# Two column blocks of the shared values by seven half-size products instead of eight

## The chip, the cores and the metric

The kernel runs on one core of a Trainium2 chip. The metric is the time of one launch in microseconds, as the median of several runs. The engines are named as in the profile: PE multiplies matrices into PSUM, DVE (VectorE) and ACT (ScalarE) work on tiles, POOL does next to nothing here, and SP issues most of the DMAs (ACT issues a few).

## The reference

A trunk of two layers over 512 tokens (T) of width 2048 (D), all in float32. Layer 0 is differential attention. After it the stream `x` is projected once to shared keys, values and forget-gate logits, and layer 1 (forgetting attention) reads these.

```python
def shared_kv(x, c_act, w_mod_kv, b_mod_kv, w_kv, b_f):
    mod = c_act @ w_mod_kv + b_mod_kv
    shift, scale = jnp.split(mod, 2, axis=-1)
    hk = x * (1.0 + scale[:, None]) + shift[:, None]
    kvf = hk @ w_kv
    k, v, zf = jnp.split(kvf, [B_WIDTH, 2 * B_WIDTH], axis=-1)
    ...
```

Each layer also has `mod = c_act @ w_mod[l] + b_mod[l]`, which gives a shift, a scale and a gate of the stream, and ends in `x <- LN(alpha * x + gate * mixer(x * (1 + scale) + shift))`.

## The kernel before

**A product.** Every projection is done as three matmuls (`products`): each operand is split into a rounded upper part (fp32r) and the rest, and upper x upper, upper x lower and lower x upper are summed in PSUM. The operand of the shared projection, `hk`, lies turned (features on the 128 partitions, P) in 16 pairs of tiles `Hh[kt]`, `Hl[kt]` of 128 x 512 tokens. `n` is the layer-normed stream of layer 0, four blocks of 128 tokens (TB).

**The weights** come through `WeightStream`. A step is two rows of 128 weights, up to 512 columns wide (512 KB). SP loads it into one of four `wst` buffers; ACT casts it to `whi` (L113) and DVE subtracts to get `wlo` (L114), three buffers of each. `get(job, s, ahead=2)` prepares the steps two ahead of the one that PE uses.

**A group** (`group`) multiplies one block of up to 512 columns: eight weight steps, in each of which PE goes over the four token blocks ("banks"), a burst of 6 matmuls for each. A whole step is 24 matmuls. With `natural` the tokens are PE's stationary side, which gives values; without it the weights are, which gives turned keys.

**The values**, `vj[0]` to `vj[4]`, are columns 0, 512 and 1024 (512 wide), 1536 and 1800 (264 wide; the last 16 are the gate logits). `vj[0]` is computed while its operands are being built: a build of half the tokens is transposes on PE, four activations on ACT (L1347, L1348) and DVE's subtractions (L1349), or, where the tokens were turned by way of a DRAM tile (`turned`), ACT's L1332 and DVE's L1331 and L1333. The turned tokens are kept in the place where `n` lay, for the later operands of layer 1 (`build_h`, L1384, in kj[3]). `vj[1]` to `vj[4]` follow as plain groups, then the keys `kj[0]` to `kj[3]`, then layer 1's own projections, `bj`.

**Background work.** `mod_stream` sums the modulation rows on DVE, a 128x512 block of weights at a time (L433, `macc<-ms`). `bg` says after which bursts one such product is done: after every second in the values, after three of four in the keys, after two of three in part of layer 0's output projection. Its blocks come through three `ms` buffers, loaded two ahead; those whose number lies in `deep` go to free tiles of the key pool (`msk`) and are loaded up to seven ahead.

**Order.** A scheduler puts each engine's instructions in order from the written program; each engine, and each issuing queue, then goes through its list and waits in place for what an instruction needs.

## Time and profile before

| | |
|---|---|
| median of 3 runs | 1925.03 us (1924.69 to 1926.31) |
| span of the profiled execution | 1923.5 us |
| PE busy / DVE / ACT | 99% / 71% / 38% of the span |
| matmuls on PE | 8921 |
| granted TensorE clock | full throughout |
| DMA traffic | 382.22 MB, 199 GB/s on average, 385 GB/s in the fullest of 40 slices |
| vj[0] with the build / vj[1] / vj[2] | 965 to 1022 / 1022 to 1064 / 1064 to 1107 us |
| vj[3] / vj[4] / kj[0] to kj[3] | 1107 to 1131 / 1131 to 1154 / 1154 to 1329 us |

Busy shares are over the whole span. PE's matmuls overlap, so their listed durations (0.39 us) are longer than the distance of their starts, and a busy PE isn't a proof that it waits for nothing; its gaps are seen in the windows. A row of the groups ends with the idle time of the engine just ahead of the group's instructions and with what ended it.

### The profile page before, as it was taken

The page shows a single profiled execution, that of the slowest core. Times are in us where ns is not written, and L with a number is a line of the kernel's source. Part 1 is how long each engine was busy: PE and PEld are TensorE (multiplying, and loading weights), DVE is VectorE, ACT ScalarE, POOL GpSimd, SP SyncE. Part 2 cuts the span into 40 slices and gives each one's busy share as a digit, 9 for nine tenths or more (in the row PEclk, how much of TensorE's full clock was granted, in tenths as well). Part 3 has the DMA queues.
Part 4 walks back from the last instruction along what each step waited for, and adds up shares of the span by engine and source line. Part 5 has one row for each costly group of instructions (what it writes and reads, how often), then busy time and mean ns, then how long its engine had stood idle before and what let it go on. Part 6 is the DMA issues. An engine that isn't in the chain of part 4 may idle for free.

```text
span 1923.5 us, 25879 instructions
## 1 busy us (share of the span) xinstructions
PE 1910.4 (99%) x8921; PEld 1593.5 (83%) x8921; DVE 1370.3 (71%) x2617; ACT 732.9 (38%) x1266; POOL 2.3 (0%) x11
## 2 busy tenths in 40 slices
PE   8999999999999999999999999999999999999998
PEld 7888888888888888888888898888888888888887
DVE  8993578777676868667675477777566666686768
ACT  3656344333232344521272232224344444453122
POOL 0000000000000000000000000000000000000000
PEclk9999999999999999999999999999999999999999
DMA  9993566676767675476557586775355555555622
GB/s 346 385 333 95 160 186 196 213 234 196 228 203 224 207 223 180 122 241 222 179 165 256 181 294 211 258 258 160 114 149 156 161 149 160 154 154 170 224 93 110
DMA packets 352275, 382.22 MB, mean 199 GB/s; under 512 B 77912, under 2 KB 256244, under 8 KB 351376
## 3 DMA queue, kind: packets, MB, share of 16 engines
q1 hardware_dynamic: 349040, 376.23, 62.2%
q10 hardware_dynamic: 3104, 4.35, 0.6%
q8 instruction: 70, 1.15, 0.3%
q14 instruction: 61, 0.50, 0.1%
HBM read 348.68 MB, written 31.80 MB: 198 GB/s over the span
## 4 chain that ended last, share of the span: by engine, by line
PE 97%; DVE 1%; SPq 1%; DMA 0%; issue 0%; ACT 0%; ACTq 0%
PE acc L208 27%; PE acc L210 27%; PE acc L209 27%; PE acc L720 4%; PE sc L720 2%; PE sc L210 1%; PE sc L209 1%; PE sc L208 1%; PE o L208 1%; PE o L210 1%; PE o L209 1%; PE o L720 1%; SPq L568 0%; PE tr L686 0%; PE tr L660 0%; DMA sms<-in_w_mod_dram 0%
## 5 line engine op out<-in xcount | busy, mean ns | idle before, releaser
L113 ACT CAST whi<-wst 128x1024 fp32r<-128x1024 f32 (+2 forms) x298 | 303.4, 1018 | 617.6 <-PE acc L210 310.1
L114 DVE TENSOR_TENSOR wlo<-wst,whi 128x1024 fp32r<-128x1024 f32 (+2 forms) x298 | 351.4, 1180 | 248.8 <-ACT whi L113 228.9
L208 PE MATMUL acc<-hh,whi 128*128 128x512 f32 x1184 | 462.9, 391 | 0.0
L209 PE MATMUL acc<-hl,whi 128*128 128x512 f32 x1184 | 461.6, 390 | 0.0
L210 PE MATMUL acc<-hh,wlo 128*128 128x512 f32 x1184 | 460.0, 390 | 0.0
L208 PE MATMUL acc<-whi,hh 128*128 128x512 f32 (+1 forms) x1104 | 418.5, 379 | 0.0
L209 PE MATMUL acc<-wlo,hh 128*128 128x512 f32 (+1 forms) x1104 | 416.7, 377 | 0.0
L210 PE MATMUL acc<-whi,hl 128*128 128x512 f32 (+1 forms) x1104 | 416.2, 377 | 0.0
L433 DVE SCALAR_TENSOR_TENSOR macc<-ms,cact,macc 128x512 f32<-128x512 f32 x307 | 229.0, 746 | 63.0 <-DMA ms<-in_w_mod_dram 44.5
L210 PEld LDWEIGHTS acc<-hh,wlo 128*128 128x128 f32 x1184 | 222.3, 188 | 47.4
L208 PEld LDWEIGHTS acc<-hh,whi 128*128 128x128 f32 x1184 | 222.3, 188 | 44.0 <-DVE sgb L1509 0.8
L209 PEld LDWEIGHTS acc<-hl,whi 128*128 128x128 f32 x1184 | 222.5, 188 | 42.3
L210 PEld LDWEIGHTS acc<-whi,hl 128*128 128x128 f32 x1104 | 207.3, 188 | 38.9
L208 PEld LDWEIGHTS acc<-whi,hh 128*128 128x128 f32 x1104 | 207.3, 188 | 37.2 <-DVE ztmp L1241 0.6
L209 PEld LDWEIGHTS acc<-wlo,hh 128*128 128x128 f32 x1104 | 207.4, 188 | 36.0
L618 DVE SCALAR_TENSOR_TENSOR sacc<-sms,cact,sacc 128x512 f32<-128x512 f32 (+1 forms) x128 | 89.9, 703 | 4.6 <-DMA sms<-in_w_mod_dram 0.7
L904 ACT ACTIVATE e<-e,mn 128x128 f32<-128x128 f32 (+3 forms) x64 | 36.0, 563 | 109.5 <-DVE mn L900 102.9
L1559 ACT ACTIVATE eb<-eb,mnb 128x128 f32<-128x128 f32 (+1 forms) x64 | 35.9, 561 | 72.7 <-DVE mnb L1556 72.4
L720 PE MATMUL acc<-wlo,hh 128*128 128x512 f32 x128 | 49.8, 398 | 0.0
L720 PE MATMUL acc<-whi,hl 128*128 128x512 f32 x128 | 49.3, 393 | 0.0
L720 PE MATMUL acc<-whi,hh 128*128 128x512 f32 x128 | 49.2, 393 | 0.0
L132 DVE TENSOR_TENSOR wlo<-wst,whi 128x768 fp32r<-128x768 f32 (+1 forms) x32 | 34.8, 1088 | 17.8 <-ACT whi L125 16.5
(336 smaller groups left out, 2096.6 us busy)
## 6 DMA issues: line engine op xcount, KB each, us to landing
wst<-in_a_w_in_dram SPq DMA_DIRECT2D x240, 256.0 KB
ms<-in_w_mod_dram SPq DMA_DIRECT2D x136, 256.0 KB
ms<-in_kv_w_mod_dram SPq DMA_DIRECT2D x64, 512.0 KB
wst<-in_b_w_in_dram SPq DMA_DIRECT2D x128, 256.0 KB
sms<-in_w_mod_dram SPq DMA_DIRECT2D x56, 512.0 KB
wst<-in_kv_w_dram SPq DMA_DIRECT2D x56, 512.0 KB
ms<-in_w_mod_dram SPq DMA_DIRECT2D x32, 512.0 KB
wst<-in_a_w_out_dram SPq DMA_DIRECT2D x32, 512.0 KB
```

What stands on the lines that cost most here:

```text
L113: self.nc.scalar.copy(hi[:, :, :w], st[:, :, :w])
L114: self.nc.vector.tensor_tensor(lo[:, :, :w], st[:, :, :w], hi[:, :, :w].bitcast(F32), op=ALU.subtract)
L132: self.nc.vector.tensor_tensor(lo[:, :, :w], st[:, :, :w], hi[:, :, :w].bitcast(F32), op=ALU.subtract)
L208: PE.matmul(dst, lhs[0], rhs[0], start=start, stop=False, skip_group_check=True)
L209: PE.matmul(dst, lhs[0], rhs[1], start=False, stop=False, skip_group_check=True)
L210: PE.matmul(dst, lhs[1], rhs[0], start=False, stop=stop, skip_group_check=True)
L433: ins = V.scalar_tensor_tensor(acc, w, cact[:, kt : kt + 1], acc, op0=ALU.mult, op1=ALU.add)
L618: V.scalar_tensor_tensor(acc, w, sc, acc, op0=ALU.mult, op1=ALU.add)
L720: PE.matmul(bank[n, bk], l, r, start=start, stop=stop, skip_group_check=True)
L904: S.activation(e[:, :w], e[:, :w], AF.Exp, bias=mn, scale=-1.0, accum_out=rs)
L1559: S.activation(e[:, :w], e[:, :w], AF.Exp, bias=mn, scale=-1.0, accum_out=rs)
```

## The change

`vj[1]` and `vj[2]` (value columns 512 to 1535) together are a product of 512 tokens x 2048 features by 2048 x 1024. Cut in halves along each side it is eight products of half-size blocks. The change computes it by seven products of sums of blocks (the scheme with fifteen additions known as Strassen-Winograd): the tokens halve into the first and last 256, the features into even and odd tiles `kt`, the columns into the two blocks of 512.

- `combine(s)` makes, for the two feature tiles of weight step s, the four sums of token halves, in DVE (four 128x256 operations) from freshly activated tiles (ACT, L1491; L1488 in halves for s = 6 and 7). For each pair of s, ACT casts the upper parts into `su` (two of L1507), and DVE subtracts the lower parts `sl` (four of L1511). `su` takes the places of `n`, which is split in four tiles by columns: each is stored to `s_dram` (1 MB) ahead and loaded back by `back_n` after the products. `sl` takes the sixteen tiles of the key pool.
- The order is now `vj[0]`, `vj[3]` (with combine(0) to (5)), `vj[4]`, then `seven_products` (with combine(6) and (7)), then the keys.
- `seven_products` goes over the weights twice, in 12 and in 16 steps of 512 KB with 12 matmuls each. In `PairFirst` the last eight steps need one sum of weights (L87, in place, ahead of the cast), in `PairSecond` every two steps need three (L108 to L110).
- Results are combined on ACT and DVE from PSUM at the ends of the passes (L1549 to L1586).
- Background products: none in `seven_products`, after every fourth burst in `vj[3]` and `vj[4]`, after every burst in the keys, after five of six in part of layer 0's output projection; `deep` holds numbers 82 to 137 rather than 50 to 105.
- `n` goes to `n_dram` in sixteen pieces of 256 KB rather than four of 1 MB.

The diff, cut to its core (lines that only pass on the splitting of `n` are left out):

```diff
+class PairFirst:
+
+    width = 512
+    gate = None
+
+    def __init__(self, src, c0, c1):
+        self.src, self.c0, self.c1 = src, c0, c1
+
+    def load(self, nc, dst, kt):
+        n = kt // 2
+        if n < 4:
+            rows = self.src[4 * n * P : (4 * n + 4) * P, self.c0 : self.c0 + 512]
+            nc.sync.dma_start(dst, rows.rearrange("(k u p) n -> p k u n", p=P, u=2)[:, :, 0, :])
+        else:
+            rows = self.src[2 * (n - 4) * P : (2 * (n - 4) + 2) * P, self.c1 : self.c1 + 512]
+            nc.sync.dma_start(dst, rows.rearrange("(k p) n -> p k n", p=P))
+
+    def sums(self, nc, n, st, after):
+        if n >= 4:
+            nc.vector.tensor_tensor(st[:, 0, :], st[:, 1, :], st[:, 0, :], op=ALU.subtract)
+
+class PairSecond:
+
+    width = 512
+    gate = None
+
+    def __init__(self, src, c0, c1):
+        self.src, self.cols = src, (c0, c1)
+
+    def load(self, nc, dst, kt):
+        n = kt // 2
+        c0 = self.cols[n % 2]
+        rows = self.src[2 * (n // 2) * P : (2 * (n // 2) + 2) * P, c0 : c0 + 512]
+        nc.sync.dma_start(dst, rows.rearrange("(k p) n -> p k n", p=P))
+
+    def sums(self, nc, n, st, after):
+        if n % 2 == 0:
+            other, minus = after(), partial(nc.vector.tensor_tensor, op=ALU.subtract)
+            minus(other[:, 0, :], other[:, 0, :], st[:, 0, :])
+            minus(other[:, 1, :], other[:, 1, :], other[:, 0, :])
+            minus(st[:, 0, :], st[:, 1, :], other[:, 1, :])
...
+        if isinstance(job, (PairFirst, PairSecond)):
+            self.load(self.done + 2)
+            job.sums(self.nc, s, st, lambda: self.stage[self.done + 1])
...
+    s_dram = dram.tile([4, P, TB, 512], F32, name="s_dram")
...
+    pair = PairFirst(kv_w, 2048 + 512, 2048 + 1024), PairSecond(kv_w, 2048 + 512, 2048 + 1024)
-    for j in [o[1] for o in oA] + vj + kj + bj + [o[1] for o in oB]:
+    for j in [o[1] for o in oA] + [vj[0], vj[3], vj[4]]:
+        ws.add_job(j)
+    for j, steps in zip(pair, (12, 16)):
+        ws.add_job(j, steps)
+    for j in kj + bj + [o[1] for o in oB]:
...
+    def new_n():
+        nt[:] = [zp[0].tile([P, TB, 512], F32, name="n", tag="n", bufs=4) for _ in range(4)]
...
-            bg = (lambda n: 1 if n % 3 else 0) if layer == 0 and k in (1, 2) else 0
+            bg = (lambda n: 1 if n % 6 else 0) if layer == 0 and k in (1, 2) else 0
...
-            deep=range(50, 106),
+            deep=range(82, 138),
...
-        for c0, c1 in ((0, 256), (256, 1024)) if b == 3 else ((0, 1024),):
-            S.activation(n[:, b, c0:c1], n[:, b, c0:c1], AF.Identity, scale=rstd, bias=mr)
-        V.tensor_scalar(n[:, b, 1024:], n[:, b, 1024:], mv[:, 0:1], rstd, op0=ALU.subtract, op1=ALU.mult)
-        nc.sync.dma_start(n_dram[b * P : (b + 1) * P, :], n[:, b, :])
+        for c0, c1 in ((0, 256), (256, 512), (512, 1024)) if b == 3 else ((0, 512), (512, 1024)):
+            S.activation(ncols(b, c0, c1), ncols(b, c0, c1), AF.Identity, scale=rstd, bias=mr)
+        for c0 in (1024, 1536):
+            row = ncols(b, c0, c0 + 512)
+            V.tensor_scalar(row, row, mv[:, 0:1], rstd, op0=ALU.subtract, op1=ALU.mult)
+        for c0 in range(0, D, 512):
+            nc.sync.dma_start(n_dram[b * P : (b + 1) * P, c0 : c0 + 512], ncols(b, c0, c0 + 512))
...
+    def combine(s):
+
+        cs = 256 * s, 256 * s + 256
+        whole = []
+        for q in range(2):
+            kt = 2 * s + q
+            f = npool.tile([P, T], F32, name="htmp", tag="htmp", bufs=2)
+            sc, sh = ab["kv"][0][:, kt : kt + 1], ab["kv"][1][:, kt : kt + 1]
+            if turned(s, 0):
+                for half in range(2):
+                    to = f[:, 256 * half : 256 * half + 256].rearrange("p (b a c) -> p b a c", b=2, c=32)
+                    S.activation(to, place_n(s, half, q), AF.Identity, scale=sc, bias=sh)
+            else:
+                src = ncols(slice(0, TB), kt * P, (kt + 1) * P)
+                S.activation(f.rearrange("p (b t) -> p b t", t=P), src, AF.Identity, scale=sc, bias=sh)
+            whole.append((f[:, 0:256], f[:, 256:512]))
+        if s % 2:
+            nc.sync.dma_start(s_dram[s // 2], nt[s // 2])
+        sums = npool.tile([P, 4, 256], F32, name="sums", tag="tn", bufs=2)
+        (a11, a21), (a12, a22) = whole
+        s3, s4, s1, s2 = (sums[:, k, :] for k in range(4))
+        V.tensor_tensor(s1, a21, a22, op=ALU.add)
+        V.tensor_tensor(s2, s1, a11, op=ALU.subtract)
+        V.tensor_tensor(s3, a11, a21, op=ALU.subtract)
+        V.tensor_tensor(s4, a12, s2, op=ALU.subtract)
+        waiting.append((s, sums))
+        if s % 2:
+            t = npool.tile([P, 2, 4, 256], F32R, name="su", tag="n", bufs=4)
+            for k, (w, sums) in enumerate(waiting):
+                upper[w] = t[:, k]
+                S.copy(upper[w], sums)
+                lower[w] = [kpool.tile([P, 2, 256], F32R, name="sl", tag="K") for _ in range(2)]
+                for m, lo in enumerate(lower[w]):
+                    two = slice(2 * m, 2 * m + 2)
+                    V.tensor_tensor(lo, sums[:, two], upper[w][:, two].bitcast(F32), op=ALU.subtract)
+            waiting.clear()
...
+    def combined(s, k, b):
+
+        bs = slice(b * P, (b + 1) * P)
+        return upper[s][:, k, bs], lower[s][k // 2][:, k % 2, bs]
...
+    def seven_products():
+
+        one, two = pair
+        c0, c1 = (c - 2048 for c in (one.c0, one.c1))
+        both = range(2)
+
+        def add(dst, lhs, tiles, k, start=False, stop=False):
+            for b in both:
+                products(dst[b], lhs(b), (tiles[0][k], tiles[1][k]), start, stop)
+
+        def store(t, b, col):
+            nc.scalar.dma_start(v_dram[b * P : (b + 1) * P, col : col + 512], t)
+
+        p1 = [acc_bank() for _ in both]
+        for a in range(4):
+            tiles = ws.get(one, a)
+            if a < 2:
+                combine(6 + a)
+            for k in range(2):
+                s = 2 * a + k
+                add(p1, lambda b: plain(2 * s, b), tiles, k, s == 0, s == 7)
+        p2 = [tr_bank("p2"), o_bank("p2")]
+        first = [npool.tile([P, T], F32, name="vfirst", tag="vfirst", bufs=2) for _ in both]
+        for b in both:
+            S.copy(first[b], p1[b])
+        p7 = [acc_bank() for _ in both]
+        p3 = [sc_bank() for _ in both]
+        for s in range(8):
+            tiles = ws.get(one, 4 + s)
+            add(p7, lambda b: combined(s, 0, b), tiles, 0, s == 0, s == 7)
+            add(p3, lambda b: combined(s, 1, b), tiles, 1, s == 0, s == 7)
+        diff = [npool.tile([P, T], F32, name="htmp", tag="htmp", bufs=2) for _ in both]
+        for b in both:
+            S.copy(diff[b], p3[b])
+            V.tensor_tensor(diff[b], p7[b], diff[b], op=ALU.subtract)
+        for s in range(8):
+            last = s == 7
+            ta = ws.get(two, 2 * s, 1)
+            add(p2, lambda b: plain(2 * s + 1, b), ta, 1, s == 0, last)
+            if s not in (0, 7):
+                add(p7, lambda b: plain(2 * s + 1, 2 + b), ta, 0)
+            tb = ws.get(two, 2 * s + 1, 1 if s in (0, 7) else 2)
+            add(p1, lambda b: combined(s, 3, b), tb, 1, stop=last)
+            if s in (0, 7):
+                add(p7, lambda b: plain(2 * s + 1, 2 + b), ta, 0, stop=last)
+            add(p3, lambda b: combined(s, 2, b), tb, 0, stop=last)
+            if last:
+                for b in both:
+                    V.tensor_tensor(first[b], p2[b], first[b], op=ALU.add)
+                    store(first[b], b, c0)
+                us = [ktile("us") for _ in both]
+                for b in both:
+                    S.copy(us[b], p1[b])
+                for b in both:
+                    t = ktile("vt")
+                    V.tensor_tensor(t, p7[b], us[b], op=ALU.add)
+                    store(t, 2 + b, c0)
+                for b in both:
+                    t = ktile("vt")
+                    V.tensor_tensor(t, p3[b], us[b], op=ALU.add)
+                    store(t, b, c1)
+                    V.tensor_tensor(diff[b], diff[b], t, op=ALU.add)
+                    store(diff[b], 2 + b, c1)
+
+    def back_n():
+        new_n()
+        for f in range(4):
+            nc.sync.dma_start(nt[f], s_dram[f])
...
-    for g in range(1, 5):
-        group(vj[g], True, evac_v(g), bg=lambda k: k % 2)
+    group(vj[3], True, evac_v(3), bg=lambda k: k % 4 == 3, after_sub=lambda s: combine(s) if s < 6 else None)
+    group(vj[4], True, evac_v(4), bg=lambda k: k % 4 == 3)
+    seven_products()
+    back_n()
...
-            pieces.extend([None] * 8 + [lambda: ab.update(b=fold(1, npool.tile([P, 512], F32, name="mrow_b", tag="mrow_b", bufs=1)))])
+            pieces.extend([None] * 12 + [lambda: ab.update(b=fold(1, npool.tile([P, 512], F32, name="mrow_b", tag="mrow_b", bufs=1)))])
-            kj[g], False, evac_k(g), bg=lambda k: 1 if k % 4 else 0,
+            kj[g], False, evac_k(g), bg=1,
```

**What moves in the engines' lists.** On ACT, in `vj[0]`, while operands are built: ahead of the change a build (L1347, L1348; L1332 for turned tokens) is followed by the next or by a cast of weights. The names: `htmp2`, `hh` are the parts of an operand, `whi` a weight step. Before:

```order
L1347 ACTIVATE htmp2_9253<-sc_9248,mod_b0_7741,mod_a0_7740 128x256
L1348 ACTIVATE hh_9146<-sc_9248,mod_b0_7741,mod_a0_7740 128x256
L1347 ACTIVATE htmp2_9257<-sc_9248,mod_b0_7741,mod_a0_7740 128x256
L1348 ACTIVATE hh_9152<-sc_9248,mod_b0_7741,mod_a0_7740 128x256
L1332 ACTIVATE hh_9274<-n_7761,mod_b0_7741,mod_a0_7740 128x256
L1332 ACTIVATE hh_9280<-n_7761,mod_b0_7741,mod_a0_7740 128x256
L113 CAST whi_9298<-wst_9105 128x1024
```

After, with the builds now L1413, L1414 and L1398 and the weight cast L162:

```order
L1414 ACTIVATE hh_9141<-sc_9243,mod_b0_7742,mod_a0_7741 128x256
L1491 ACTIVATE htmp_9512<-n_7763,mod_b0_7742,mod_a0_7741 128x512
L1491 ACTIVATE htmp_9514<-n_7763,mod_b0_7742,mod_a0_7741 128x512
L1507 CAST su_9522<-sums_9474 128x1024
L1398 ACTIVATE hh_9269<-n_7766,mod_b0_7742,mod_a0_7741 128x256
L162 CAST whi_9293<-wst_9128 128x1024
L1398 ACTIVATE hh_9275<-n_7766,mod_b0_7742,mod_a0_7741 128x256
```

Two activations of combine(1) and the cast of combine(0)'s sums stand between two builds and ahead of a cast of weights.

On DVE, at the passage from the first to the second pass of `seven_products` (`wst` a loaded step, `wlo` its lower part, L1559 the differences of two PSUM results); nothing like it stands in the list before, where `vj[2]` has one subtraction for each step and background products:

```order
L163 TENSOR_TENSOR wlo_10251<-wst_10187,whi_10250 128x1024
L87 TENSOR_TENSOR wst_10254<-wst_10254 128x512
L163 TENSOR_TENSOR wlo_10270<-wst_10216,whi_10269 128x1024
L163 TENSOR_TENSOR wlo_10289<-wst_10235,whi_10288 128x1024
L108 TENSOR_TENSOR wst_10292<-wst_10292,wst_10273 128x512
L109 TENSOR_TENSOR wst_10292<-wst_10292 128x512
L163 TENSOR_TENSOR wlo_10308<-wst_10254,whi_10307 128x1024
L110 TENSOR_TENSOR wst_10273<-wst_10273,wst_10292 128x512
L163 TENSOR_TENSOR wlo_10329<-wst_10273,whi_10328 128x1024
L108 TENSOR_TENSOR wst_10332<-wst_10332,wst_10311 128x512
L163 TENSOR_TENSOR wlo_10347<-wst_10292,whi_10346 128x1024
L109 TENSOR_TENSOR wst_10332<-wst_10332 128x512
```

L87 of a step stands ahead of the subtraction of the step two before, and the sums of the second pass stand between the last subtractions of the first.

On DVE, in `kj[2]`, the background products (`macc`) between two weight steps (`wlo`). Before:

```order
L114 TENSOR_TENSOR wlo_11477<-wst_11350,whi_11476 128x1024
L433 SCALAR_TENSOR_TENSOR macc_11414<-ms_11464,cact_101,macc_11414 128x512
L433 SCALAR_TENSOR_TENSOR macc_11414<-ms_11473,cact_101,macc_11414 128x512
L433 SCALAR_TENSOR_TENSOR macc_11414<-ms_11494,cact_101,macc_11414 128x512
L114 TENSOR_TENSOR wlo_11516<-wst_11389,whi_11515 128x1024
```

After:

```order
L163 TENSOR_TENSOR wlo_11730<-wst_11593,whi_11729 128x1024
L488 SCALAR_TENSOR_TENSOR macc_11612<-ms_11699,cact_102,macc_11612 128x512
L488 SCALAR_TENSOR_TENSOR macc_11612<-ms_11708,cact_102,macc_11612 128x512
L488 SCALAR_TENSOR_TENSOR macc_11612<-ms_11717,cact_102,macc_11612 128x512
L163 TENSOR_TENSOR wlo_11772<-wst_11649,whi_11771 128x1024
```

One more product stands ahead of each weight step.

More of the change, by code (lines that the diff above doesn't have):

```diff
@@ L83, in add, with add_job @@
         self.order.append((job, sub))
-    def add_job(self, job):
-        for s in range(KT // 2):
+    def add_job(self, job, steps=KT // 2):
+        for s in range(steps):
             self.add(job, s)
@@ L1128, in place_n @@
     def place_n(s, half, q):
-        return zp[1][:, 2 * half + q, 2 * s * P : (2 * s + 2) * P].rearrange("p (a b c) -> p b a c", b=2, c=32)
+        return ncols(2 * half + q, 2 * s * P, (2 * s + 2) * P).rearrange("p (a b c) -> p b a c", b=2, c=32)
     pieces.append(lambda: evac_qk(1)(3, raw["k1"]))
@@ L1238, in sums @@
                 def sums():
-                    zs = z[:, b, 512 * f : 512 * (f + 1)]
+                    zs = z[:, b, 512 * f : 512 * (f + 1)] if layer else ncols(b, 512 * f, 512 * (f + 1))
                     tmp = pool.tile([P, 512], F32, name="ztmp", tag="htmp", bufs=2)
@@ L1307, in norm_a @@
     def norm_a(b, _):
-        pool, n, stats = zp
+        pool, _, stats = zp
         mv, rstd = moments(pool, stats, b)
@@ L1337, in build_half @@
             for b in range(2):
-                src = n[:, 2 * half + b, (2 * s + q) * P : (2 * s + q + 1) * P]
+                src = ncols(2 * half + b, (2 * s + q) * P, (2 * s + q + 1) * P)
                 PE.transpose(px[:, q * 256 + b * P : q * 256 + (b + 1) * P], src, ident)
@@ L1349, in build_half @@
             V.tensor_tensor(Hl[kt][:, hs], tmp, Hh[kt][:, hs].bitcast(F32), op=ALU.subtract)
-        place = n[:, 2 * half : 2 * half + 2, 2 * s * P : (2 * s + 2) * P].rearrange("p b (q t) -> p q b t", t=P)
+        place = ncols(slice(2 * half, 2 * half + 2), 2 * s * P, (2 * s + 2) * P).rearrange("p b (q t) -> p q b t", t=P)
         V.tensor_copy(place, px.rearrange("p (q b t) -> p q b t", q=2, b=2))
@@ L1403, in fn @@
             if nv < w:
-                fz["cols", b] = vt[:, nv:w]
-        return fn
+                S.copy(fcols[:, b, :], vt[:, nv:w])
+                fz["cols", b] = fcols[:, b, :]
+        return fn
+    fcols = npool.tile([P, TB, B_HEADS], F32, name="fcols")
+    upper, lower = {}, {}
+    def combine(s):
[33 more added lines that the diff above has]
+            waiting.clear()
@@ new lines, in tile_yoco, with plain @@
+    waiting = []
+    def combined(s, k, b):
+        bs = slice(b * P, (b + 1) * P)
+        return upper[s][:, k, bs], lower[s][k // 2][:, k % 2, bs]
+    def plain(kt, b):
+        bs = slice(b * P, (b + 1) * P)
+        return Hh[kt][:, bs], Hl[kt][:, bs]
+    def seven_products():
[57 more added lines that the diff above has]
+                    store(diff[b], 2 + b, c1)
```

20 lines of the change are left out of this document (12 added, 8 removed).

## The prediction

> **What bounds the kernel now.** I read the page first: its engine shares and the chain that ended last.
>
> ```profile
> span 1923.5 us, 25879 instructions
> PE 1910.4 (99%) x8921; PEld 1593.5 (83%) x8921; DVE 1370.3 (71%) x2617; ACT 732.9 (38%) x1266; POOL 2.3 (0%) x11
> PE 97%; DVE 1%; SPq 1%; DMA 0%; issue 0%; ACT 0%; ACTq 0%
> ```
>
> The chain of waits lies on PE for 97% of the span, so a matmul less is a gain, unless something else becomes late. The matmul rows read 0.39 us each, but they overlap; PE's timeline gives the step that counts:
>
> ```profile
> 1284.89 0.39 PE L210 MATMUL acc<-hh,wlo 128*128 128x512 f32 x1
> 1285.11 0.39 PE L208 MATMUL acc<-hh,whi 128*128 128x512 f32 x1
> 1285.34 0.39 PE L209 MATMUL acc<-hl,whi 128*128 128x512 f32 x1
> 1285.57 0.39 PE L210 MATMUL acc<-hh,wlo 128*128 128x512 f32 x1
> ```
>
> Three starts in 0.68 us: 0.227 us a matmul. A weight step of 24 takes 5.44 us, one of 12 takes 2.72 us. Next the windows by stage (us, then PE, PEld, DVE, ACT, POOL busy, clock, DMA share, GB/s):
>
> ```profile
> 965.00:1022.00 57.00, 56.78 (x271) 46.45 (x270) 40.43 (x95) 39.85 (x71) 0.00 (x0) 1.00 0.52 162
> 1022.00:1064.00 42.00, 42.00 (x187) 34.79 (x186) 22.37 (x27) 11.26 (x14) 0.00 (x0) 1.00 0.78 261
> 1064.00:1107.00 43.00, 43.00 (x193) 35.63 (x192) 21.22 (x26) 9.32 (x13) 0.00 (x0) 1.00 0.57 193
> 1107.00:1131.00 24.00, 24.00 (x203) 24.00 (x202) 18.03 (x26) 7.25 (x14) 0.00 (x0) 1.00 0.87 292
> 1131.00:1154.00 23.00, 23.00 (x190) 22.80 (x189) 19.06 (x26) 7.04 (x13) 0.00 (x0) 1.00 0.89 296
> 1285.00:1329.00 44.00, 44.00 (x196) 36.17 (x195) 38.15 (x67) 19.19 (x27) 0.00 (x0) 1.00 0.56 182
> ```
>
> The first row is vj[0] with the build of its operands, then vj[1], vj[2] (the two that are replaced), vj[3], vj[4]; the last is kj[3]. PE is full at clock 1.00 in all of them, while DVE is half idle beside vj[1] and vj[2]. What the new work costs comes from the groups by shape in 965 to 1329:
>
> ```profile
> L114 DVE TENSOR_TENSOR wlo<-wst,whi 128x1024 fp32r<-128x1024 f32 x57 | 69.6, 1220 | 46.2 <-ACT whi L113 46.2
> L433 DVE SCALAR_TENSOR_TENSOR macc<-ms,cact,macc 128x512 f32<-128x512 f32 x88 | 65.9, 749 | 26.6 <-DMA ms<-in_w_mod_dram 25.2
> L114 DVE TENSOR_TENSOR wlo<-wst,whi 128x528 fp32r<-128x528 f32 x16 | 11.3, 707 | 16.1 <-ACT whi L113 11.9 <-DMA msk<-in_w_mod_dram 4.1
> L1349 DVE TENSOR_TENSOR hl<-htmp,hh 128x256 fp32r<-128x256 f32 x24 | 10.0, 417 | 7.2 <-ACT hh L1348 7.2
> L204 DVE TENSOR_TENSOR hl<-htmp,hh 128x512 fp32r<-128x512 f32 x14 | 9.5, 686 | 2.5 <-PE acc L209 2.5
> L113 ACT CAST whi<-wst 128x1024 fp32r<-128x1024 f32 x57 | 60.0, 1053 | 156.3 <-PE acc L209 87.1 <-PE acc L210 60.0 <-issue 4.3
> L1347 ACT ACTIVATE htmp<-sc,mod_b,mod_a 128x256 f32<-128x256 f32 x24 | 13.4, 560 | 3.8 <-PE sc L1339 2.4 <-DVE hl L1349 1.4
> L1314 ACT ACTIVATE n<-n,mr,lrstd 128x768 f32<-128x768 f32 x1 | 1.0, 1014 | 0.0
> L1400 ACT COPY vt<-acc 128x264 f32<-128x264 f32 x8 | 3.0, 378 | 2.3 <-PE acc L210 2.2
> ```
>
> **What goes.** Eight half-size products of 48 matmuls become seven: 384 become 336, all of 128x512. 48 x 0.227 = 10.9 us is the whole gain, if PE never waits. Weight steps go from 16 of 5.44 us to 28 of 2.72 us, so each loaded megabyte is used for half as long, and every load, cast and subtraction has half the cover.
>
> **vj[0]: combine(0) and combine(1).** The scheduler puts the four 512-wide activations (L1491) and the cast of `su` (L1507) between the builds. ACT is busy 39.85 of 57 us there, and DVE's part of an operand comes just in time:
>
> ```profile
> 1008.81 0.42 DVE L1349 TENSOR_TENSOR hl<-htmp,hh 128x256 fp32r<-128x256 f32 x1
> 1009.95 0.39 PE L210 MATMUL acc<-whi,hl 128*128 128x512 f32 x1
> ```
>
> `hl` ends at 1009.23 and is used at 1009.95: 0.7 us ahead. Between 256 wide (0.56) and 768 wide (1.01) an activation of 512 is about 0.8 us, so two of them and the cast (1.05) put 2.6 us in front of the next build. Less 0.7 us, this is at most 1.9 us late; with ACT idle a third of the time (57 less 39.85), I take 1.0 us, with 0 and 2.6 as ends. The store of `n` to `s_dram` that the cast must wait for is issued more than ten ACT instructions sooner, and is costed at nothing; should it be late, `su` holds the weight casts queued behind it, and PE.
>
> **vj[3] and vj[4].** DVE has in these 47 us 16 subtractions of 0.707, 14 background products of 0.749, 24 sums like L1349 (0.417), 10 subtractions for `sl` like L204 (0.686) and two more of 0.7: 11.3 + 10.5 + 10.0 + 6.9 + 1.4 = 40.1 us. It was 18.03 + 19.06 = 37.1. It fits; 0, at most 2.
>
> **The pair, start.** Whi and wlo have three buffers each: a step's pair is written when PE ends the step three back, and two steps (5.44) less cast and subtraction (1.05 + 1.22) leave 3.2 us of lead, where steps of 24 leave 8.6. The first `sl` tiles need the K tiles that held vj[4]'s evacuated values, so they wait for four stores issued after PE ends vj[4]; DVE has them ahead of the third step's wlo. Nearest rows for store latency are the small loads below, 3.4 us at best: copy 0.38 + 3.4 + two `sl` 1.3 + wlo 1.22 = 6.3 us after the pair starts, against a use at 5.44 + 0.45 (PE's third matmul needs wlo) = 5.9. Late by 0.4 us, and the following steps keep about 0.9 us of lead rather than 3.2.
>
> **The pair, first pass.** A load of 512 KB, an in-place subtraction (L87), then the split: before has this very sequence near the end, with a gate in place of the subtraction.
>
> ```profile
> 1846.50 0.37 SPq L63 DMA_DIRECT2D wst<-in_b_w_out_dram  x1
> 1850.20 1.29 DVE L104 TENSOR_TENSOR wst<-wst,gate 128x512 f32<-128x512 f32 x2 [1.08 <-DMA wst<-in_b_w_out_dram]
> 1852.66 0.37 SPq L63 DMA_DIRECT2D wst<-in_b_w_out_dram  x1
> 1856.24 0.69 DVE L104 TENSOR_TENSOR wst<-wst,gate 128x512 f32<-128x512 f32 x1 [2.28 <-DMA wst<-in_b_w_out_dram]
> 1856.85 1.22 DVE L114 TENSOR_TENSOR wlo<-wst,whi 128x1024 fp32r<-128x1024 f32 x1
> ```
>
> Issue to use is 3.70 and 3.58 us, the operation takes 0.61 to the next start. In DVE's order L87 of step s stands ahead of wlo of step s-2, whose end lets the load of step s+2 go: 3.6 + 0.6 + 1.22 = 5.4 us for two steps, and PE takes 5.44. Balanced: it loses nothing, and gains nothing back. [...]
>
> **The pair, passage and second pass.** The first three sums of pass two (L108 to L110) stand in DVE's queue between the last wlo of pass one, and each waits for a load let go by the wlo before. From the end of wlo(9): load 3.6, L108 and L109 1.2, wlo(11) 1.2, L110 0.6, cast 1.1, wlo 1.2, meanwhile the next load (3.6 after wlo(11)) and L108, wlo, L109, the two PSUM differences (L1559, 0.6 each), L110, cast 1.1, wlo: 16.8 us to the third step of pass two, where PE comes after five steps, 13.6. Short 3.2 us, less the lead of 0.9: 2.3. Beyond, sums, cast and two splits come to 1.8 + 1.1 + 2.4 = 5.3 for 5.44. So the pair costs 0.4 + 2.3 and some 0.3 for semaphores, 3.0 us; ends 0 (stores land early and lead stays 3.2) and 6 (loads of 4.4 us). The four reloads of `n` wait for PE work that is over before the weight loads behind them on SP's queue are let go: 0.
>
> **Keys and background sums.** What the values stage no longer does of the modulation sums, kj does at four a step rather than three. Up to kj[1] they were loaded far ahead; after that, 54 loads through three `ms` buffers stand ahead of 14 weight steps. An `ms` load now:
>
> ```profile
> 1257.37 1.03 SPq L409 DMA_DIRECT2D ms<-in_w_mod_dram  x1
> 1262.35 0.75 DVE L433 SCALAR_TENSOR_TENSOR macc<-ms,cact,macc 128x512 f32<-128x512 f32 x1 [1.25 <-DMA ms<-in_w_mod_dram]
> 1263.13 0.33 SPq L409 DMA_DIRECT2D ms<-in_w_mod_dram  x1
> 1266.88 0.75 DVE L433 SCALAR_TENSOR_TENSOR macc<-ms,cact,macc 128x512 f32<-128x512 f32 x1 [1.06 <-DMA ms<-in_w_mod_dram]
> 1267.66 0.33 SPq L409 DMA_DIRECT2D ms<-in_w_mod_dram  x1
> 1271.06 0.75 DVE L433 SCALAR_TENSOR_TENSOR macc<-ms,cact,macc 128x512 f32<-128x512 f32 x1
> 1275.29 1.22 DVE L114 TENSOR_TENSOR wlo<-wst,whi 128x1024 fp32r<-128x1024 f32 x1 [1.39 <-ACT whi L113]
> ```
>
> 3.40 to 3.75 us from issue to use, and 4.98 when a weight load went just before. Three buffers give (L + 0.75) / 3 per product. The wlo of 1276.5 is used by PE at 1285.57, 9.05 us later: that is the cover. 14 x 5.44 + 9.05 = 85.2 us are there for 54 products: L may be 3.98. One in four follows a weight load: (3 x 3.7 + 4.98) / 4 = 4.0. I take 4.05, a stall of 1.2 us, with the builds in kj[3] (DVE 38.15 of 44 us already) adding 0.3: 1.5 us. Ends 0 and 9.5 (L = 4.5).
>
> **Sum.** -10.9 + 1.0 + 0 + 3.0 + 1.5 = -5.4. The profiled execution took 1923.5 in span; the median of the runs, 1925.03, has 1.5 more around it, which I leave. 1925.03 - 5.4 = 1919.6, said as 1919.5.
>
> **Rivals.** (A) The waits are hidden. Loads 0.3 us faster than the rows above would win back the lead in pass one and keep the ring within 85 us; only vj[0]'s 1.0 and the start's 0.4 stay: 1915.5. For it: all three links are within 0.1 us of balance. Against: no row of a 512 KB load shows under 3.5 us. [...] (B) The gain is eaten by weight loads: next to 8.4 MB of `s_dram` traffic and 6.3 MB of additional weights a load takes 4.5, 0.9 more in four turns of pass one and twice in the passage: 5.4 us more, 1925. For it: the first `ms` row; against: vj[1] and vj[2] ran at 261 and 193 GB/s, and two loads in 5.44 us are 193. (C) Slower: the ring of `ms` buffers. At L = 4.98 for all, 54 x 5.73 / 3 = 103 us against 85.2: 18 us on PE in kj[2] to bj[0], 1936. It decides from L = 4.55, 10 us, which takes the time over 1929. For it: DVE already waited 25.2 us for `ms` with three a step; against: those waits were made while it was ahead. (D) The products don't shorten PE because DVE sets the pace in both passes: less likely, as 5.4 is under 5.44; it falls within B.
>
> **Chances.** Forecast, 1918 to 1922: 0.36. A, under 1918: 0.22. B, 1922 to 1929: 0.25. C, over 1929: 0.17. About 0.2% (3.85 us) can be told from no change: faster means below 1921.2, slower above 1928.9. Faster: 0.22 and most of 0.36, 0.53; same: 0.30; slower: 0.17. The range runs from 1914.5, all but 0.4 us of the gain, to 1929.
>
> **What would show it.** PE idle in the window of vj[0] up by about 1 us; DVE waiting for stores ahead of the first `sl` at the pair's start; 2 to 3 us of PE idle waiting on wlo at the passage, none in pass two; L87 waiting for its load each time, 3.6 us after issue; wlo's lead in kj[2] shrinking from 9 us, and PE idle at bj[0]'s start if at all. Wrong if loads there take under 3.3 or over 4.5 us, or if ACT, not DVE, is the late one.

## The result and the profile after

The changed kernel is slower: 1953.10 us median of 4 runs (1948.06 to 1955.61) against 1925.48, ratio 1.0138 [1.0126, 1.0151]; 27.6 us. The head of its page and the chain's shares:

```profile
span 1953.8 us, 26045 instructions
PE 1914.0 (98%) x8873; PEld 1588.9 (81%) x8873; DVE 1430.2 (73%) x2723; ACT 764.7 (39%) x1312; POOL 2.3 (0%) x11
PE 80%; DMA 9%; DVE 7%; issue 2%; ACT 1%; SPq 0%; DVEq 0%; ACTq 0%
```

The 48 matmuls are gone (8921 to 8873), yet the chain, which lay on PE for 97%, now lies on DMA for 9% and on DVE for 7%. PE waits in places where it did not wait before. The list of its waits (us in total, times, longest):

```profile
PE acc L258 <- DVE ztmp L1303: 6.9, 3, 4.5
PE tr L529 <- DVE mred L520: 4.2, 1, 4.2
PE tr L1631 <- DVE rows L1625: 3.8, 1, 3.8
PE acc L258 <- ACT kT L1459: 3.7, 4, 1.6
...
PE acc L259 <- DVE wlo L163: 2.5, 4, 1.0
PE p L259 <- DVE wlo L163: 1.8, 2, 1.1
...
PE acc L258 <- ACT vt L1466: 1.7, 1, 1.7
```

None of these rows stands in the same list of before. Where the time went, from four places in the PE timelines (us; the last two columns are experiments told below):

| | before | after | e1_ms5 | e11_copies |
|---|---|---|---|---|
| first transposes of the build | 964.4 | 974.5 | 963.9 | 964.6 |
| from there to the first key matmul (values stage) | 188.5 | 191.0 | 189.6 | 184.5 |
| from there to kj[1]'s first copy out of PSUM | 84.5 | 91.3 | 87.3 | 85.3 |
| from there to the last matmul | 680.5 | 690.8 | 680.9 | 681.0 |

The four differences of after and before, 10.2 + 2.5 + 6.9 + 10.3, make up the 29.8 us (each is rounded) by which the last matmul is late (this execution took 1955.61 us, 2.5 over the median). Ten of them are lost before the stage that the change is about: in layer 0's output projection, from 834 us on, where DVE's waits now read:

```profile
DVE macc L488 <- DMA ms<-in_w_mod_dram: 24.9, 18, 3.5
```

and for the same stretch of before:

```profile
DVE macc L433 <- DMA ms<-in_w_mod_dram: 12.7, 9, 3.2
```

The chain through that stretch (start, us, what) is loads of 256 KB, one after the other, with DVE between them, until PE stands. The twelve loads on it take 2.7 to 5.5 us, 4.4 on average; three of them:

```profile
877.83 2.72 DMA ms<-in_w_mod_dram
...
893.52 4.95 DMA ms<-in_w_mod_dram
...
926.68 5.07 DMA ms<-in_w_mod_dram
931.84 0.75 DVE macc L488
932.99 0.61 DVE ztmp L1303
933.74 0.76 PE acc L258
```

`ztmp` (L1303) is DVE's copy of the projection's results out of PSUM. It stands in DVE's queue behind the products, and PE can't begin the next bank before it. The tile's own view gives the pace of the ring:

```profile
L464 SPq DMA_DIRECT2D ms<-in_w_mod_dram x49: 327/328/418, 844.9 to 933.0; - x49
```

From the first to the last of 49 loads are 48 steps in 88.1 us, 1.84 us each. With three buffers that is 5.5 us a turn: 0.75 for the product, and 4.75 for the load and what else DVE does in between. A burst of PE takes 6 x 0.227 = 1.36 us; one product after two bursts of three asks for one in 2.04 us, which the ring can give; after five of six it is one in 1.63, which it can't.

The stall itself is not all of it. PE's timeline around it:

```profile
928.80 0.39 PE L260 MATMUL acc<-whi,hl 128*128 128x512 f32 x1
933.74 0.76 PE L258 MATMUL acc<-whi,hh 128*128 128x512 f32 x1 [4.55 <-DVE ztmp L1303]
934.30 0.63 PE L259 MATMUL acc<-wlo,hh 128*128 128x512 f32 x1
934.73 0.63 PE L260 MATMUL acc<-whi,hl 128*128 128x512 f32 x1
```

Two windows of after (us, then PE, PEld, DVE, ACT, POOL busy, clock, DMA share, GB/s):

```profile
930.00:974.30 44.30, 40.56 (x167) 33.36 (x168) 32.10 (x69) 9.80 (x14) 0.00 (x0) 0.92 0.54 177
...
1348.00:1362.00 14.00, 7.46 (x27) 5.00 (x26) 12.88 (x24) 6.93 (x11) 0.00 (x0) 0.90 0.50 161
```

From 928.80 to 933.74, 4.94 us, no matmul starts, and the next ones start 0.43 us apart, not 0.227, while the window has clock 0.92: a dozen matmuls so, 0.2 us lost on each, some 2.5 on top of the stall. It comes again at the end of the keys (clock 0.90 in the second window), and for six matmuls in kj[0].

### The profile page after: what moved, and what is told of

Same layout as the page of the kernel before. It is cut to its first block, busy times and chain, and to the rows that moved or that the text cites. A ratio compares the mean times of both kernels' runs of the same rounds, so it can differ in the third digit from the quotient of the medians.

```text
span 1953.8 us, 26045 instructions
## 1 busy us (share of the span) xinstructions
PE 1914.0 (98%) x8873; PEld 1588.9 (81%) x8873; DVE 1430.2 (73%) x2723; ACT 764.7 (39%) x1312; POOL 2.3 (0%) x11
## 4 chain that ended last, share of the span: by engine, by line
PE 80%; DMA 9%; DVE 7%; issue 2%; ACT 1%; SPq 0%; DVEq 0%; ACTq 0%
PE acc L258 21%; PE acc L259 21%; PE acc L260 20%; DMA ms<-in_w_mod_dram 6%; PE acc L775 5%; PE sc L775 2%; DVE macc L488 2%; DMA wst<-in_kv_w_dram 2%; DVE wlo L163 2%; PE sc L259 1%; PE sc L260 1%; PE sc L258 1%; PE o L258 1%; PE o L260 1%; PE o L775 1%
## 5 line engine op out<-in xcount | busy, mean ns | idle before, releaser
L162 ACT CAST whi<-wst 128x1024 fp32r<-128x1024 f32 (+2 forms) x310 | 314.8, 1018 | 600.4 <-PE acc L260 239.2
L163 DVE TENSOR_TENSOR wlo<-wst,whi 128x1024 fp32r<-128x1024 f32 (+2 forms) x310 | 365.3, 1181 | 205.5 <-ACT whi L162 192.3
L259 PE MATMUL acc<-hl,whi 128*128 128x512 f32 x1184 | 463.5, 391 | 0.0
L258 PE MATMUL acc<-whi,hh 128*128 128x512 f32 (+1 forms) x1008 | 383.2, 380 | 9.6 <-DVE ztmp L1303 6.9
L259 PE MATMUL acc<-wlo,hh 128*128 128x512 f32 (+1 forms) x1008 | 380.5, 378 | 0.3 <-DVE wlo L163 0.3
L260 PE MATMUL acc<-whi,hl 128*128 128x512 f32 (+1 forms) x1008 | 379.5, 377 | 0.4 <-DVE hl L1399 0.4
L259 PEld LDWEIGHTS acc<-hl,whi 128*128 128x128 f32 x1184 | 223.6, 189 | 42.6
L258 PEld LDWEIGHTS acc<-whi,hh 128*128 128x128 f32 x1008 | 189.9, 188 | 46.0 <-issue 5.8
L260 PEld LDWEIGHTS acc<-whi,hl 128*128 128x128 f32 x1008 | 189.7, 188 | 36.3 <-DVE hl L1399 1.2
L259 PEld LDWEIGHTS acc<-wlo,hh 128*128 128x128 f32 x1008 | 190.1, 189 | 33.0 <-DVE wlo L163 0.7
```

Of the source, the lines that this page charges most:

```text
L162: self.nc.scalar.copy(hi[:, :, :w], st[:, :, :w])
L163: self.nc.vector.tensor_tensor(lo[:, :, :w], st[:, :, :w], hi[:, :, :w].bitcast(F32), op=ALU.subtract)
L258: PE.matmul(dst, lhs[0], rhs[0], start=start, stop=False, skip_group_check=True)
L259: PE.matmul(dst, lhs[0], rhs[1], start=False, stop=False, skip_group_check=True)
L260: PE.matmul(dst, lhs[1], rhs[0], start=False, stop=stop, skip_group_check=True)
```

## The experiments

The theory after the result (1): the whole loss is the ring of three `ms` buffers, asked for products faster than it can load them, in the output projection and in the keys; the seven products by themselves gain little, since waits eat most of the 10.9 us. The rival (2): the products' own traffic and DVE work cost the time, and the modulation waits only move it.

**More buffers for `ms`.** 

```diff
-            while n < len(todo) and n <= (k + 7 if n in deep else k + 2 // nk):
+            while n < len(todo) and n <= (k + 7 if n in deep else k + (4 if nk == 1 else 2 // nk)):
...
-            lambda: pool.tile([P, 512], F32, name="ms", tag="ms", bufs=3),
+            lambda: pool.tile([P, 512], F32, name="ms", tag="ms", bufs=5),
```

(The place comes from a smaller `mrow_b` and from `vfirst` sharing a tile.)

> The changed kernel with five buffers for the background blocks (ms) and loads four ahead, rather than three and two; the place comes from a smaller mrow_b and from a vfirst tile that lies in mturn's. Theory 1 (the ring of three ms buffers is too short for the new rates: a product per (latency + 0.75)/3, with latencies of 4 to 5.5 us): the 10 us that the output projection lost go almost wholly, and of the 20 us lost in the keys some 12: 1930 to 1936. Theory 2 (the losses come from DVE's total work or from DMA traffic, and the waits for ms are only where they show): within 4 us of the changed kernel's 1953.

Measured 1929.39 us (1928.41 to 1932.03), ratio 1.0022 [1.0012, 1.0031]. Two more buffers give 24 us back, a little more than theory 1 said, and the output projection is where it was (963.9). Its list of PE's waits no longer has `ztmp`, and `mred` is down from 4.2 to 0.2:

```profile
PE acc L259 <- DVE wlo L163: 2.3, 3, 1.1
PE acc L258 <- ACT vt L1466: 1.7, 1, 1.7
PE acc L258 <- ACT kT L1459: 1.4, 1, 1.4
PE tr L1631 <- DVE rows L1625: 1.4, 1, 1.4
```

**The rate alone, in the kernel before.**

```diff
-            bg = (lambda n: 1 if n % 3 else 0) if layer == 0 and k in (1, 2) else 0
+            bg = (lambda n: 1 if n % 6 else 0) if layer == 0 and k in (1, 2) else 0
```

> The kernel before, with one edit of the change alone: background products after five of six bursts in two groups of layer 0's output projection rather than two of three. Theory 1: the output projection becomes longer as it did in the change, 8 to 11 us, and since fewer products are left for later nothing is won back: 1933 to 1936. Theory 2 (the output projection of the changed kernel is slow for another of its edits, n in four tiles with sixteen stores): 1925, no change.

Measured 1946.68 us, ratio 1.0108 [1.0093, 1.0123]: one digit, with no product of sums anywhere, costs 21.5 us, twice what was expected; by its trace the first transposes of the build come 16.8 us later than in before. PE's idle time and the clock run on into the build:

```profile
930.00:974.00 44.00, 41.13 (x172) 33.33 (x173) 23.53 (x35) 8.72 (x11) 0.00 (x0) 0.96 0.45 149
974.00:1000.00 26.00, 19.77 (x85) 15.34 (x84) 21.68 (x80) 15.34 (x26) 0.00 (x0) 0.87 0.61 222
```

**No loads of `ms`.** In both kernels every product of layer 1's modulation reads one block that is loaded once.

```diff
+            if nk == 1 and loaded_once:
+                loaded[k] = loaded_once[0]
+                return
```

> The kernel before without the loads of layer 1's modulation blocks: every background product reads one resident block (the modulation is then wrong). Theory 1: nothing on PE waited for those loads before, so within 3 us of 1925. Theory 2 (DMA traffic slows the weights as well): 5 us or more faster.

> The changed kernel without the loads of layer 1's modulation blocks, as in the run above (the modulation is then wrong). Theory 1: all of the output projection's 10 us and nearly all of the keys' 20 go; what stays is the gain of 10.9 and the losses of the value stage itself (vj[0] 2.7, vj[3] 1.8, the pair 6.6) and some of kj[0]: 1925 to 1930, within 4 us of the kernel before without loads. Theory 2 (DVE's work): over 1940. Theory 3 (the pair's waits also come from the traffic of those loads): under 1922.

Measured: before so changed 1925.26 us, 1.0001 [0.9991, 1.0010]; after so changed 1925.52, 1.0000 [0.9990, 1.0009]. Before loses nothing to these loads, after all of its 27.6 us. DVE's products are still all there in both, so it is the loads and not DVE's work that cost the time; and since e1_ms5 keeps every load, 24 of the 27.6 us are the ring's and not the traffic's. Without the loads the change is worth nothing either way: the gain of 10.9 us is lost elsewhere, and the next runs look for it.

**The rate undone, in the changed kernel**, with three buffers still.

```diff
-            bg = (lambda n: 1 if n % 6 else 0) if layer == 0 and k in (1, 2) else 0
+            bg = (lambda n: 1 if n % 3 else 0) if layer == 0 and k in (1, 2) else 0
```

> The changed kernel with the background rate in layer 0's output projection put back to two of three bursts, three ms buffers as in the change; the modulation's fold must then come 12 bursts later. Theory 1 (the ring of three buffers is short wherever the rate is above one product per 1.6 us): the output projection gains its 10 us, but the ten or so products left over come behind the keys at 1.6 us each, where the ring is already late: 1943 to 1955. Theory 2 (that rate is the one bad edit, the rest is harmless): 1926 to 1932.

Measured 1945.32 us, 1.0098 [1.0085, 1.0112]. The projection is back, and the keys, which have more products left, lose it:

```profile
PE acc L258 <- ACT kT L1459: 5.1, 4, 2.7
PE acc L260 <- DVE wlo L163: 5.0, 1, 5.0
```

So it is not one digit that is wrong: three buffers carry the products that the values stage gave up neither with the faster rate in the projection nor with more of them left to the keys.

**DVE's order in the pair**, with the five buffers. L87 of a step is put ahead of the subtraction of the step one before, rather than two, and the first sums of pass two behind the last subtraction of pass one.

```diff
+            if isinstance(job, PairFirst) and s < 11:
+                self.early.add(self.done + 1)
+                job.sums(self.nc, s + 1, self.stage[self.done + 1], None)
...
-            self.nc.vector.tensor_tensor(lo[:, :, :w], st[:, :, :w], hi[:, :, :w].bitcast(F32), op=ALU.subtract)
+            ins = self.nc.vector.tensor_tensor(lo[:, :, :w], st[:, :, :w], hi[:, :, :w].bitcast(F32), op=ALU.subtract)
+            if isinstance(job, (PairFirst, PairSecond)):
+                self.keep(ins)
```

> The changed kernel with five ms buffers (the run e1_ms5, 1929.4) and the order of DVE in the pair held by hand: the in-place sum of a step stands one step ahead of the subtraction of the step before it, not two, and the sums of pass two behind the last subtraction of pass one. The same instructions. Theory 1 (a load sits between two subtractions that are only two steps of 2.72 us apart, so a load of 4 to 5 us sets the pace): three steps apart it has room, and most of the 4 us that PE loses in the pair go: 1925 to 1927. Theory 2 (the loads take long because of traffic, or DVE's work in the pair is too much, whatever its order): 1929.

Measured 1925.88 us, 0.9999 [0.9990, 1.0008], 3.5 us less than with the buffers alone (4.2 less when each is held against the runs of before beside it, 1925.86 and 1925.19); the values stage is 185.4 us instead of 189.6. PE's waits for `wlo` went from the 2.5 and 1.8 us of after (2.3 and 1.0 with the buffers alone) to 0.2:

```profile
PE acc L266 <- DVE wlo L168: 0.2, 1, 0.2
```

**Two tries at the rest.** e9_best pins combine(6) and (7) and their `su` and `sl` behind single steps of the pair and starts the columns of the forget gate 16 bursts later; e10_all pins the activations of combine(0) to (5) as well.

```diff
-                S.activation(f.rearrange("p (b t) -> p b t", t=P), src, AF.Identity, scale=sc, bias=sh)
+                tc.keep_in_program_order(S.activation(f.rearrange("p (b t) -> p b t", t=P), src, AF.Identity, scale=sc, bias=sh))
```

> As e5_order, with the activations and sums of combine(6) and (7) held behind the third and fifth weight step of the pair, their split into su and sl two steps later each, and the transposes of the forget sums 16 bursts later in kj[0]. Theory 1: the start of the pair no longer waits for stores of vj[4] ahead of a weight step, vj[4] no longer starts behind activations (1.8 us), PE doesn't wait for the forget sums (1.8 us): 1920 to 1924. Theory 2 (what is moved is only late elsewhere): as e5_order.

> As e9_best, and the activations of combine(0) to (5) held in the order in which they are written, which takes combine(0) and (1) out of vj[0] and its builds. Theory 1: vj[0] wins back its 2 to 3 us, vj[3] and vj[4] have room for it (41 of 47 us on DVE): 1917 to 1922, faster than the kernel before. Theory 2: vj[3] and vj[4] lose what vj[0] wins: as e9_best.

Measured 1925.27 us, 0.9998 [0.9989, 1.0006], and 1929.85, 1.0022 [1.0012, 1.0031]. In neither did theory 1 hold. In e10_all vj[0] has lost nearly all of its gaps, but vj[4] now starts behind an `su` cast that waits for DVE. ACT's timeline there, then PE's:

```profile
1048.79 1.05 ACT L1522 CAST su<-sums 128x1024 fp32r<-128x1024 f32 x1 [1.58 <-DVE sums L1510]
1049.74 0.65 ACT L1475 COPY vt<-acc 128x264 f32<-128x264 f32 x2
```

```profile
1044.47 0.28 PE L267 MATMUL acc<-whi,hl 128*128 128x264 f32 x1
1050.17 0.59 PE L265 MATMUL acc<-whi,hh 128*128 128x264 f32 x1 [5.42 <-ACT vt L1475]
```

e9_best keeps a smaller stall of the same kind where the keys pass from one group to the next; again ACT's timeline, then PE's:

```profile
1196.13 1.04 ACT L164 CAST whi<-wst 128x1024 fp32r<-128x1024 f32 x1 [4.96 <-PE acc L266]
1197.08 2.05 ACT L1468 COPY kT<-acc 128x512 f32<-128x512 f32 x4
```

```profile
1197.71 0.50 PE L265 MATMUL acc<-hh,whi 128*128 128x512 f32 x1 [1.39 <-ACT kT L1468]
```

ACT waits 4.96 us for PE to end kj[0], to cast a later weight step, and the four copies that PE needs stand behind that cast.

**The copies ahead of the cast** (e11_copies, built on e9_best; the casts around the ends of vj[3] and kj[0] are pinned likewise).

```diff
-            S.copy(KTs[4 * g + b], acc)
+            ins = S.copy(KTs[4 * g + b], acc)
+            if g == 0:
+                tc.keep_in_program_order(ins)
```

> The kernel of e9_best, with ACT's order pinned at two more places: the four copies of vj[3] out of PSUM (vt) and the four of kj[0] (kT) stand ahead of the cast of the weight step that waits for PE to end the group. In e9_best PE waits 1.28 us at the start of vj[4] and 1.78 us at the start of kj[1] there. Theory 1 (those stalls come from a cast that stands ahead of the copies and waits for PE itself): both gaps fall under 0.5 us, 2 to 3 us less than e9_best, 1922 to 1924 us. Theory 2 (the copies are late for another reason, or the time comes back in later waits): 1925 to 1926 us, as e9_best.

Measured 1923.39 us (1922.75 to 1924.88, 11 runs), 0.9991 [0.9982, 1.0000]. The waits for `kT` are gone, that for `vt` is 0.6 us. It is the fastest kernel here that computes the reference, 2 us under before, at the edge of what its interval can tell.

**The stationary operand.** In the pair of after, matmuls with `su` or `sl` start 0.234 us apart on average, those with `hh` or `hl` 0.229 (gaps over 0.26 us left out).

```diff
-        return upper[s][:, k, bs], lower[s][k // 2][:, k % 2, bs]
+        return plain(2 * s + k % 2, b + k // 2)
```

> The kernel of e11_copies, in which the matmuls of the seven products take rounded parts of plain tokens as their stationary operand in place of the sums su and sl (the sums are still made, but what comes out of these products is another number). Same instructions on every engine, so only where the stationary operand lies differs. Question: why matmuls in the pair start 0.232 to 0.235 us apart rather than 0.227. Theory 1 (the place of su and sl in memory, written at the time by ACT and DVE): the pair runs at 0.227 us a matmul and is 1.5 to 2 us shorter than in e11_copies. Theory 2 (loading weights and writing sums at the same time, whatever the operand, or the alternation of banks): the distance stays over 0.231 us and the time is that of e11_copies within 0.5 us.

PE's timeline of e11_copies, then of e12_plain, in the first pass:

```profile
1090.26 0.39 PE L268 MATMUL acc<-whi,su 128*128 128x512 f32 x1
...
1091.89 0.40 PE L269 MATMUL sc<-wlo,su 128*128 128x512 f32 x1
```

```profile
1090.19 0.39 PE L268 MATMUL acc<-whi,hh 128*128 128x512 f32 x1
...
1091.78 0.39 PE L269 MATMUL sc<-wlo,hh 128*128 128x512 f32 x1
```

Seven steps from start to start take 1.63 us (0.233 each) against 1.59 (0.227). The distance is as theory 1 has it, but over 192 such matmuls it makes only about 1 us, and the time, 1923.17 us, 0.9990 [0.9981, 0.9999], doesn't show it: the start of vj[4] waited 0.5 us longer in this profile, and the pass 0.7 us for a cast. Both theories were half right: with the other operand the distance is 0.227 us rather than 0.233, and that is not worth a measurable time.

## Why the prediction was wrong

Forecast 1919.5 (1914.5 to 1929), measured 1953.1, outside the range and on the other side.

- **The step that failed is one that wasn't in the sum.** The change to five bursts of six in layer 0's output projection stands in the list of what changes, and the prediction prices the products only in the keys, from the end of kj[1] on. What they cost in the projection is at nothing in the sum, and no reason is given for that. In the change the first transposes come 10.2 us late; e2_rate, that digit alone in the kernel before, costs 21.5 us. Undoing it in the change (e8_rate_undone) gives back only 7.8, since the products then come in the keys.
- **Keys and background sums: 1.5 us was taken, and what failed is the cover, not L.** From kj[1]'s first copy to the end the change loses 10.3 us, of which e1_ms5 gives back 9.9. The 54 products are there, and from 1271 to 1352 us their loads go out 1.62 us apart, which with three buffers is an L of 4.1, DVE's other work in it, where 4.05 was taken. But the prediction let PE wait on `wlo` alone, with 9.05 us to spare. PE's waits at the end of the keys are on other work in the same queue, which had no such cover: 2.4 us on `kT` copies (ACT has them behind casts that wait for DVE's operand builds) and 4.2 on `mred`, DVE's closing sum behind the last product. DVE's timeline there, then PE's:

```profile
1355.48 0.75 DVE L488 SCALAR_TENSOR_TENSOR macc<-ms,cact,macc 128x512 f32<-128x512 f32 x1 [1.07 <-DMA ms<-in_w_mod_dram]
...
1359.46 0.67 DVE L520 TENSOR_REDUCE mred<-mturn 128x16 f32<-128x512 f32 x1
```

```profile
1360.29 0.39 PE L529 MATMUL tr<-fours,mred 128*64 128x32 f32 x2 [4.19 <-DVE mred L520]
```

  Rival C (chance 0.17) names this ring. Its 18 us for kj[2] to bj[0], with L = 4.98, are too many for these 10.3; that kj[0] loses 6.9 more, ahead of where C starts, and the two add to 17.2, is luck. The loads of the output projection, not those of the keys, are as slow as the first row quoted for C (4.75 against 4.98). (The DVE lists ahead of the prediction show three products between two weight steps both before and after; over the whole of kj[2] it is mostly three before and four after, as the sentence under them says.)
- **The load time.** The twelve loads of 256 KB on the projection's chain take 4.4 us on average (2.7 to 5.5), where the prediction's rows have 3.40 to 3.75 and, next to a weight load, 4.98. No run here shows what makes them longer.
- **The matmuls behind a stall** weren't priced: from 933.7 to 939.4 us they start 0.43 us apart, at clock 0.50, and that is some 2.5 us in the projection alone.
- **The gain**: 48 matmuls did go, at 0.227 us. Instead of winning these 10.9 us the values stage is 2.5 longer, so 13.4 are lost in it: gaps over 0.4 us between starts are 9.5 more than in before (vj[0] 2.2, the start of vj[4] 1.75, the pair 5.5), and the other 3.9 are shorter gaps and matmuls that start further apart.
- **vj[0]**: 1.0 taken, ends 0 to 2.6; 2.2 measured, for the reason given (ACT; e10_all removes nearly all of these gaps by ACT's order).
- **vj[3] and vj[4]**: DVE does fit, as said. The 1.75 us are ACT's: the `vt` copies stand behind activations of combine(6), an `su` cast and a weight cast, which the prediction did not look at; e9_best and e11_copies bring the wait from 1.7 to 1.0 and 0.6 by order alone.
- **The pair**: 3.0 taken, ends 0 to 6, measured 5.5: 0.5 at the start, 4.1 from 1107 to 1126 us, around the passage, where 2.3 was taken, and 0.9 late in pass two where none was. The 0.3 for semaphores was the author's estimate, and no run shows it by itself. (The steps listed for the passage add up to about 16.1 us rather than 16.8, which would have made its part 1.6; and in the pair `wlo` is needed by the second matmul, L259, not the third, 0.2 us sooner.) The first `sl` wait for stores as foretold (1.2 and 1.3 us, PE 0.5 late for 0.4 forecast). Pass one was said to be balanced with loads of 3.6 us. DVE's timeline of after:

```profile
1085.37 0.69 DVE L1511 TENSOR_TENSOR sl<-sums,su 128x512 fp32r<-128x512 f32 x1 [1.30 <-DMA v_dram<-vt]
...
1087.72 1.22 DVE L163 TENSOR_TENSOR wlo<-wst,whi 128x1024 fp32r<-128x1024 f32 x1
...
1093.85 0.69 DVE L87 TENSOR_TENSOR wst<-wst 128x512 f32<-128x512 f32 x1 [1.97 <-DMA wst<-in_kv_w_dram]
...
1099.99 1.22 DVE L163 TENSOR_TENSOR wlo<-wst,whi 128x1024 fp32r<-128x1024 f32 x1
...
1106.32 0.69 DVE L87 TENSOR_TENSOR wst<-wst 128x512 f32<-128x512 f32 x1 [2.68 <-DMA wst<-in_kv_w_dram]
```

  From the end of a `wlo` to the L87 that it lets load: 4.9 and 5.1 us in these rows, 3.7 to 5.1 and 4.5 on average over the five L87 that wait. That is the load of rival B (4.5, 5.4 us more). Its reason, more traffic, isn't shown: from 1090 to 1110 us the DMAs move 186 and 152 GB/s, less than the 261 and 193 beside vj[1] and vj[2] in before. The prediction's reading of the queue was right: e5_order undoes just that order and gets 4.2 us back in the values stage.
- **Not in the sum at all**: kj[0]'s forget-gate sums and the `kT` copies. They cost 2.8 us in kj[0] even with five buffers.
- With the waits shortened that the runs above go after, e11_copies keeps 4.0 of the 10.9 us in the values stage and 2 of the whole.

## What to carry to other kernels

When a change takes background work out of one stage, ask where it goes, and divide: a ring of b buffers gives one product in (load + use) / b (here three buffers gave one in 1.84 us, and the loads of 4.4 us on average with 0.75 of use make 1.7), to be held against the rate now asked for, in every stage whose rate was touched, with the load time of the busiest row. Then ask what else stands behind these products in the same queue: the 9 us of cover that one wait had were no cover for the others. A small digit in a rate can cost more than the arithmetic that it makes room for (21.5 us in e2_rate, against 10.9 for the 48 matmuls). And before the copies out of PSUM at the end of a group, look at what stands ahead of them in ACT's or DVE's queue: a cast that waits for PE itself cost 1.4 us at the end of kj[0] in e9_best.

## What the runs showed of the hardware

The PE idles of 3.85, 4.19 and 4.55 us in after cost more than themselves: the next matmuls start 0.43 us apart rather than 0.227, as in the rows at 934 us, and the windows of these three stretches have clock 0.52, 0.51 and 0.50. PE's timeline of kj[0] shows the end of one:

```profile
1191.98 0.57 PE L1631 MATMUL tr<-ident,rows 16*128 16x16 f32 x4 [3.85 <-DVE rows L1625]
...
1194.78 0.63 PE L258 MATMUL acc<-hh,whi 128*128 128x512 f32 x1
1195.21 0.47 PE L259 MATMUL acc<-hl,whi 128*128 128x512 f32 x1
1195.52 0.39 PE L260 MATMUL acc<-hh,wlo 128*128 128x512 f32 x1
```

Here it ends 3.4 us after PE began again; behind the stall at 934 us it lasts 5.7, to 939.4, and behind the wait for `mred` 5.9, to 1366.2. Other runs have such a stretch behind a shorter idle. In the profiled execution of e4_after_noload (1929.23 us, 3.7 over that run's median) a stretch follows an idle of 1.54 us, and the window from 1020 to 1026 us has clock 0.72:

```profile
1020.70 0.68 PE L258 MATMUL acc<-whi,hh 128*128 128x512 f32 x1 [1.54 <-ACT hh L1404]
1021.18 0.63 PE L259 MATMUL acc<-wlo,hh 128*128 128x512 f32 x1
1021.61 0.63 PE L260 MATMUL acc<-whi,hl 128*128 128x512 f32 x1
```

In e2_rate idles of 2.85 and 2.22 us have such a stretch behind them, while in after the 1.7 us at the start of vj[4] and in e8_rate_undone 2.73 us in the keys have none. So in these runs the length of one idle doesn't tell whether such a stretch follows; what does stays open.

And in e11_copies, from 1090.26 us on, matmuls whose stationary operand is `su` or `sl` start 0.233 us apart; in e12_plain, with `hh` or `hl` in that place, 0.227, with the same weight load time (188 ns in both). Which property of these tiles does it (their place, how they are written or what they hold) stays open, and they aren't the only ones: the first ten steps of the pair in after, with `hh` or `hl`, take 2.32 us, 0.232 each.
